# A pooling stage between two FFNs: boundary chain first on every engine, gate rows and weight low parts in its gaps, bias by float32r matmuls of two parts

## The chip, the cores and the metric

The kernel runs on one core of a Trainium2 chip. The metric is device time in microseconds of one execution; a kernel's time is the median of its runs. A profile is one further execution with the hardware profiler on.

## What is computed

A two-layer encoder trunk over 256 tokens of 1024 channels, all in float32. Each layer is FFN, token mixer, FFN. The mixer of layer 0 pools, that of layer 1 is latent attention. Every sub-layer has a norm before and after and is shifted, scaled and gated by rows computed from a vector `c`.

```python
def pool_mixer(h, w, b, scale):            # group g: window 2, 4, 8, 16; 256 channels each
    ...
    y = jnp.einsum('bsgc,gcd->bsgd', pooled - hg, w) + b
    return y.reshape(B, S, D_MODEL) * scale

def modulated_sublayer(x, mod, g_pre, g_post, fn, weight):
    shift, scale, gate = mod[:, 0], mod[:, 1], mod[:, 2]
    h = rmsnorm(x, g_pre) * (1.0 + scale) + shift
    y = rmsnorm(fn(h), g_post)
    return x + weight * (1.0 + gate) * y
...
    mod = (sc @ ada_w[i] + ada_b[i]).reshape(B, N_MOD, D_MODEL)[:, :, None, :]
```

## The kernel before

Tokens are two tiles of 128 (t = 0, 1), with x resident in SBUF. A product in float32 accuracy is made of three float32r matmuls: each operand is split into a high part (a cast on ScalarE, ACT) and a low part (operand minus high part, on VectorE, DVE), and TensorE (PE) adds high x high, high x low and low x high (`mm3`, lines L98 to L100). Weights arrive as 1 MB pieces: `wi` of the FFN's input (chunk c, half q of the inner dimension: wi00, wi01, wi10, ...), `wo` of its output, `ada` for the modulation rows. Each piece is a task of the class `Bulk`: load (a DMA on SP's queue into one of `N_RAW` = 4 raw buffers), high part, low part. When a piece's last work on DVE is written down, `advance()` writes the next load into SP's queue; that load then waits on the chip until DVE has read the buffer that it overwrites. The split parts lie in a ring of 12 buffers (`hl_tile`).

The modulation rows are made on DVE: `ada_step` (L352) adds one row of `ada_w` times a value of `c`. The tasks ("ada", 0, 7, 2) and ("ada", 0, 7, 3), ada2 and ada3 for short, are the last two pieces of the scale row of the next FFN.

The code order is the order on each engine; nothing is rescheduled, and each engine runs its instructions strictly in that order. SP's queue too is in code order.

A boundary between two sub-layers is a chain for each tile: sums of squares of the sub-layer's output on ACT (`post_sq`, L508), the norm's factor (`rstd`: DVE L501, then GpSimd L503), x updated on DVE (L535 to L538), squares of x on ACT (L508), factor again, x scaled into `xr` (one half on ACT L554, the other on DVE L555), transposed on PE (`turn_half`, L562, into `ps_h`), modulated into `hs` (one half on ACT L576, the other on DVE L582), split into `hTH` (L588, L590) and `hTL` (L593). The next matmuls need hTH and hTL.

The stage of the change lies between the first FFN `f0` and the second, `f2`. `FFN.tail` of f0 ends with tile 0's chain, during which tile 1's last matmuls run; its arguments `next_weights`, `between` and `between2` put extra work into it. Then the pooling: `pool_map` multiplies hT by the group weights `pw` into `z` (PE, L98 to L100), ACT copies z to SBUF (L1466, L1481, L1482), `pool_bias` puts the bias row into the accumulators `accp` by a plain float32 matmul with one row of ones (L954), `pool_mix` adds the pooling as a plain float32 matmul with the matrix `mix` (L965), `pool_scale_rows` multiplies by `pool_scale` into `pooly` (DVE, L979). `rows_of_gate` makes the gate row G (PE L448, DVE L456, L457), `reduce_held` sums rows over partitions by one-column matmuls (`ps_mod`, L361), and `warm` issues matmuls into a scratch bank that nobody reads (L108). Then follow tile 0's chain and `FFN.head` of f2, which starts with `in00` (chunk 0, tile 0) on PE while tile 1's chain runs. Constants of the stage, `mix`, `pool_b` and `pool_scale`, are loaded by `pool_consts` (L926, L928, L929); `pool_b` and `pool_scale` share the buffer `poolbs`.

Of the kernel before, what the change touches and what calls it, by code (L numbers as in the profile page):

```python
# [39 lines left out]
def kernel(  # L40
# [387 lines left out]
    def gate(layer, sub, hold=None, in_parts=True):  # L428
# [15 lines left out]
        def half(acc, dst, hf, ps, halves=None, staged=None):  # L444
# [10 lines left out]
            def after():  # L455
                nc.vector.tensor_add(dst[:, sl], ps if staged is None else dst[:, sl], rows[2 * hf])  # L456
                nc.vector.scalar_tensor_tensor(  # L457
                    dst[:, sl], dst[:, sl], 1.0, rows[2 * hf + 1], op0=ALU.add, op1=ALU.mult
                )
# [1220 lines left out]
```

## Time and profile before

| | |
|---|---|
| median of 3 runs | 925.95 us (924.56 to 929.2) |
| the profiled execution | 930.35 us, of which the span from its first to its last instruction is 928.6 us |
| mean granted TensorE clock | 0.990 |
| busy: PE, DVE, ACT, GpSimd | 97%, 76%, 47%, 5% of the span |
| DMA | 235.28 MB, mean 253 GB/s |

Rows of the timeline read: start, duration, engine, line, operation, tile written and tiles read, shape, count. A row x4 merges four records; a plain float32 matmul leaves two records. A bracket at a row's end is idle time of its engine in front of it, and what ended it. Adjacent records of one engine overlap a little, since one is issued before the other has drained.

### The profile page before, as it was taken

What the parts mean: (1) busy time and instruction counts of PE and PEld (TensorE: products, weight loads), DVE (VectorE), ACT (ScalarE), POOL (GpSimd) and SP (SyncE); (2) the same over time, 40 slices, a digit from 0 to 9 for tenths busy, and PEclk for the clock granted to TensorE, in tenths of its full rate; (3) what the DMA queues carried; (4) which work ended last, traced back from release to release, by engine and by line L of the source; (5) the groups of instructions that cost most, each with busy time, mean ns of one, the idle gap of its engine ahead of it and who ended that gap; (6) DMA issues with size and microseconds to landing.
All of it is one profiled execution on the core that took longest, in us unless ns stands there. A gap on an engine that the chain in (4) does not pass through costs nothing.

```text
span 928.6 us, 11171 instructions
## 1 busy us (share of the span) xinstructions
PE 898.9 (97%) x4251; PEld 733.0 (79%) x4251; DVE 703.9 (76%) x848; ACT 437.3 (47%) x653; POOL 41.8 (5%) x56
## 2 busy tenths in 40 slices
PE   3999999999999999999999999999999999999997
PEld 3568887887888888888888888888776888888885
DVE  5798888887877898797867987766798765656553
ACT  2255443345645434334742534337698654343421
POOL 0000000000000000000000000001163000000000
PEclk9899999999999999999999999998999999999999
DMA  9989998996357999898469999961143458857601
GB/s 325 368 299 343 360 373 313 351 359 242 137 180 264 378 339 326 297 387 275 137 183 360 324 351 327 344 229 59 46 137 113 160 153 280 293 193 259 227 1 45
DMA packets 135973, 235.28 MB, mean 253 GB/s; under 512 B 5628, under 2 KB 98415, under 8 KB 135664
## 3 DMA queue, kind: packets, MB, share of 16 engines
q1 hardware_dynamic: 135920, 234.58, 72.8%
q8 instruction: 33, 0.54, 0.2%
q14 instruction: 20, 0.16, 0.1%
HBM read 233.51 MB, written 1.05 MB: 253 GB/s over the span
## 4 chain that ended last, share of the span: by engine, by line
PE 88%; DVE 7%; issue 2%; DMA 1%; ACT 1%; POOL 0%; SPq 0%; DVEq 0%; POOLq 0%; ACTq 0%
PE acc L747 25%; PE in L100 16%; PE in L98 16%; PE in L99 16%; PE accm L1319 2%; PE ps_g L724 2%; DVE aacc L352 1%; PE ps_h L562 1%; PE ps_mod L361 1%; PE in L794 1%; DVE nm L1220 1%; DVE ql L1203 1%; DMA wo<-in_ffn_w_out_dram 1%; PE accp L965 1%; DMA adah<-in_ada_w_dram 1%
## 5 line engine op out<-in xcount | busy, mean ns | idle before, releaser
L352 DVE SCALAR_TENSOR_TENSOR aacc<-ada,sc,aacc 128x1024 f32<-128x1024 f32 (+1 forms) x113 | 143.8, 1272 | 9.9 <-DMA ada<-in_ada_w_dram 7.6
L708 ACT ACTIVATE sil<-in 128x256 f32<-128x256 f32 x84 | 32.2, 383 | 247.0 <-PE in L100 242.1
L710 DVE TENSOR_TENSOR g<-in,sil 128x256 f32<-128x256 f32 x84 | 35.2, 419 | 52.0 <-ACT sil L708 51.9
L95 DVE TENSOR_TENSOR gL<-ps_g,gH 128x256 fp32r<-128x256 f32 x88 | 36.6, 416 | 23.6 <-ACT gH L94 23.5
L94 ACT CAST gH<-ps_g 128x256 fp32r<-128x256 f32 x88 | 32.4, 368 | 44.5 <-PE ps_g L724 44.4
L503 POOL TENSOR_TENSOR r<-ms,mhalf 128x1 f32<-128x1 f32 x24 | 13.6, 565 | 840.5 <-DVE ms L501 840.5
L724 PEld LDWEIGHTS ps_g<-ident,g 128*128 128x128 f32 x176 | 24.7, 140 | 11.5
L724 PE MATMUL ps_g<-ident,g 128*128 128x128 f32 x176 | 33.6, 272 | 0.0
L508 ACT ACTIVATE junk<-x 128x512 bf16<-128x512 f32 x24 | 15.1, 631 | 21.1 <-DVE x L535 11.3
L361 PE MATMUL ps_mod<-ones,aacc 128*128 128x1 f32 x96 | 12.9, 262 | 10.9 <-DVE cols L150 9.7
L361 PEld LDWEIGHTS ps_mod<-ones,aacc 128*128 128x128 f32 x96 | 13.2, 213 | 11.9 <-DVE cols L150 10.0
L576 ACT ACTIVATE hs<-ps_h,mod,mod 128x128 f32<-128x128 f32 x48 | 18.0, 456 | 8.6 <-DVE mod L377 5.5
L352 DVE SCALAR_TENSOR_TENSOR aacc<-adah,sc,aacc 128x512 f32<-128x512 f32 x28 | 21.0, 751 | 0.9
L582 DVE TENSOR_SCALAR hs<-ps_h,mod,mod 128x128 f32<-128x128 f32 x48 | 16.4, 403 | 4.9 <-PE ps_h L562 4.6
L535 DVE SCALAR_TENSOR_TENSOR x<-tmp,r,x 128x512 f32<-128x512 f32 x23 | 16.3, 748 | 2.2 <-POOL r L503 1.2
L1238 POOL TENSOR_SCALAR p<-p,rs 128x256 f32<-128x256 f32 x16 | 16.1, 1008 | 26.8 <-ACT p L1228 16.4
L1228 ACT ACTIVATE p<-s,nm 128x256 f32<-128x256 f32 x32 | 15.0, 478 | 4.0 <-DVE nm L1220 2.6
L554 ACT ACTIVATE xr<-x,r 128x512 f32<-128x512 f32 x12 | 8.7, 722 | 17.4 <-POOL r L503 17.4
L593 DVE TENSOR_TENSOR hTL<-hs,hTH 128x512 fp32r<-128x512 f32 x24 | 15.6, 689 | 0.4
L271 DVE TENSOR_TENSOR wo10L<-wo,wo10H 128x2048 fp32r<-128x2048 f32 x4 | 9.2, 2292 | 8.1 <-ACT wo10H L263 8.1
L397 DVE TENSOR_REDUCE mod<-ps_turn 128x4 f32<-128x512 f32 x12 | 8.2, 687 | 8.1 <-PE ps_turn L391 8.1
L562 PE MATMUL ps_h<-ident,xr 128*128 128x128 f32 x96 | 13.7, 283 | 0.5 <-ACT xr L554 0.3
(498 smaller groups left out, 2880.3 us busy)
## 6 DMA issues: line engine op xcount, KB each, us to landing
wi<-in_ffn_w_in_dram SPq DMA_DIRECT2D x176, 512.0 KB, 5.8
ada<-in_ada_w_dram SPq DMA_DIRECT2D x64, 1024.0 KB, 7.1
wo<-in_ffn_w_out_dram SPq DMA_DIRECT2D x44, 1024.0 KB, 6.4
adah<-in_ada_w_dram SPq DMA_DIRECT2D x6, 1024.0 KB, 10.3
mwo<-in_mla_w_o_dram SPq DMA_DIRECT2D x4, 1024.0 KB, 6.1
bc<-in_ada_b_dram SPq DMA_DIRECT2D x12, 256.0 KB, 6.8
bc<-in_norm_g_dram SPq DMA_DIRECT2D x12, 256.0 KB, 7.4
adah<-in_ada_w_dram SPq DMA_DIRECT2D x4, 512.0 KB, 11.7
```

The costliest lines, as they stand in the source:

```text
L94: nc.scalar.copy(h, src)
L95: nc.vector.tensor_sub(lo, src, h.bitcast(F32))
L98: nc.tensor.matmul(ps, lhsT=lh, rhs=rh, start=first, stop=False)
L99: nc.tensor.matmul(ps, lhsT=lh, rhs=rl, start=False, stop=False)
L100: nc.tensor.matmul(ps, lhsT=ll, rhs=rh, start=False, stop=last)
L352: nc.vector.scalar_tensor_tensor(acc, w, sc[:, k : k + 1], acc, op0=ALU.mult, op1=ALU.add)
L361: nc.tensor.matmul(ps[:, j : j + 1], lhsT=acc[:, (j - j0) * P : (j - j0 + 1) * P], rhs=ones[:, 0:1], start=True, stop=True,)
L562: nc.tensor.transpose(ps[:, j * P : (j + 1) * P], xr[:, kk * P : (kk + 1) * P], ident)
L708: nc.scalar.activation(sil, ps[:, 0:CW], AF.Silu)
L710: nc.vector.tensor_mul(g, ps[:, CW : 2 * CW], sil)
L724: nc.tensor.transpose(ps[:, a * P : (a + 1) * P], g[:, a * P : (a + 1) * P], ident)
L747: nc.tensor.matmul(acc[hf], lhsT=lhs[:, a, :], rhs=rhs[:, a, hf * 512 : (hf + 1) * 512], start=f, stop=l)
```

## The change

It reorders the stage and changes a few forms. In f0's tail, the second ada2 piece is done earlier, `pool_consts` and the first quarter of ada3 come after it, and the new `pool_bias_split` splits the bias row into two float32r parts, which `pool_bias` then adds by two float32r matmuls for each half. Tile 1's chain goes ahead of the mixing on PE; high and low parts of wi00 and wi01, the gate rows and quarters of ada3 move into places between the chain's steps. `pre_scale` can give ACT the second half of `xr` (`act_half`), `mod_half` can let each engine cast its own half (`own`), and the first matmuls of every `FFN.head` take all high parts of hT first and the low part last (`low_last`). Most `warm` matmuls go.

```diff
@@ pre_scale, mod_half
-    def pre_scale(t, r):
+    def pre_scale(t, r, act_half=0):
         xr = rowp.tile([P, D], F32, tag="xr", name=f"xr{t}")
-        nc.scalar.activation(xr[:, 0:512], xt[t][:, 0:512], AF.Copy, scale=r)
-        nc.vector.tensor_scalar(xr[:, 512:1024], xt[t][:, 512:1024], r, None, op0=ALU.mult)
+        a, v = (slice(hf * 512, (hf + 1) * 512) for hf in (act_half, 1 - act_half))
+        nc.scalar.activation(xr[:, a], xt[t][:, a], AF.Copy, scale=r)
+        nc.vector.tensor_scalar(xr[:, v], xt[t][:, v], r, None, op0=ALU.mult)
...
-            if on_act:
+            if on_act != own:
                 nc.vector.tensor_copy(hh[:, bsl, :], hv)
@@ FFN.mm_in
+            if low_last:
+                todo = [(hh, i, k) for k in ks for i in range(2)] + [(hl, 0, k) for k in ks]
+                for n, (lhs, i, k) in enumerate(todo):
+                    rhs = self.wi[c, k // 4][i][:, k % 4, :]
+                    nc.tensor.matmul(ps, lhsT=lhs[:, k, :], rhs=rhs, start=n == 0 and k == 0, stop=False)
+                return
...
-            ps = self.inn(0, 0, hT0)
+            ps = self.inn(0, 0, hT0, low_last=True)
@@ pool_bias
-    def pool_bias(t):
-        acc = acc_tile(t, f"accp{t}")
-        for hf in range(2):
-            nc.tensor.matmul(
-                acc[hf],
-                lhsT=ones[0:1, :],
-                rhs=pool_st["bs"][0:1, hf * 512 : (hf + 1) * 512],
...
+    def pool_bias(t, acc, hf):
+        for i, part in enumerate(pool_st["b"]):
+            nc.tensor.matmul(
+                acc[hf], lhsT=ones_r[0:1, :], rhs=part[0:1, hf * 512 : (hf + 1) * 512], start=i == 0, stop=False
+            )
+
+    def pool_bias_split():
+        b = pool_st["bs"][0:1, 0:D]
+        hl = hl_tile("poolb")
+        bh, bl = hl[:, 0:D], hl[:, D : 2 * D]
+        nc.scalar.copy(bh[0:1, :], b)
+        nc.vector.tensor_sub(bl[0:1, :], b, bh[0:1, :].bitcast(F32))
+        pool_st["b"] = (bh, bl)
@@ the stage
-    def last_ada2():
+    def to_pool_map():
+        to_pool()
+        bulk.low_part(ada2, 0, 1, False)
+
+    def ahead():
         pool_consts()
-        bulk.low_part(ada2, 1, 2, True, 512, D)
+        bulk.low_part(ada3, 0, 1, False, 0, 512)
 
     hT0 = ffn_tail(
-        f0, hT, 0, 0, 0, 1, to_pool,
-        between=lambda: bulk.low_part(ada2, 0, 1, False),
-        between2=(lambda: bulk.low_part(ada2, 1, 2, False, 0, 512), last_ada2),
+        f0, hT, 0, 0, 0, 1, to_pool_map,
+        between=lambda: bulk.low_part(ada2, 1, 2, True),
+        between2=(ahead, pool_bias_split),
     )
...
-    rows_of_gate = held["pool"]([psum.tile([P, 512], F32, tag="in", name=f"ps_row{hf}") for hf in range(2)])
-    rows_of_gate([0])
-    accp0 = pool_bias(0)
+    nc.scalar.copy(*z0[1])
+    bulk.low_part(ada3, 0, 1, False, 512, D)
+    rows_of_gate = held["pool"](acc_tile(1, "ps_row"))
+    r = rstd(s2, 1.0)
+    rows_of_gate([0], (0,))
+    xr = pre_scale(1, r, 1)
+    bulk.low_part(ada3, 1, 2, False, 0, 512)
+    accp0 = acc_tile(0, "accp0")
+    for hf in range(2):
+        pool_bias(0, accp0, hf)
+    hT1 = new_hT(1)
+    h0, l0, _ = mod_half(1, 0, turn_half(1, 0, xr), hT1, 0, 1, False, True)
+    h1, l1, _ = mod_half(1, 1, turn_half(1, 1, xr), hT1, 0, 1, True, True)
     pool_mix(accp0, 0, 0)
...
+    bulk.low_part(wi(0, 0), 0, 2048, True)
     pool_mix(accp0, 0, 1)
-    pool_mix(accp1, 1, 0, (2, 3))
+    after = [reduce_held(0, 6, psum.tile([P, 512], F32, tag="in", name="ps_mod06"))]
+    accp1 = acc_tile(1, "accp1")
+    pool_bias(1, accp1, 0)
+    pool_bias(1, accp1, 1)
+    after += [reduce_held(0, 7, psum.tile([P, 512], F32, tag="in", name="ps_mod07"))]
+    pool_mix(accp1, 1, 0)
     pool_mix(accp1, 1, 1)
-    more = warm(0, "in", 2)
-    after = [reduce_held(0, 6)]
-    more(2)
-    after += [reduce_held(0, 7)]
-    more(6)
     y0 = pool_scale_rows(0, accp0)
...
+    bulk.low_part(wi(0, 1), 0, 1024, False)
+    r = rstd(s2, 1.0)
     y1 = pool_scale_rows(1, accp1, (0,))
-    xr = pre_xr(0, s2)
+    xr = pre_scale(0, r, 1)
...
+    warm(2, "in", 2)
+    h0()
+    h1()
+    l0()
+    l1()
+    ss = post_sq(y1, 1.0)
+    bulk.low_part(wi(0, 1), 1024, 2048, True)
+    f2.high_in(1, 0)
```

On SP's queue, in f0's tail, the loads stood so before (wi_1575 is wi00, wi_1617 is wi01, wi_1704 is wi10; ada_1517 is ada2 and ada_1569 is ada3):

```order
L291 DMA ada_1517<-in_ada_w_dram 128x2x1024
L291 DMA ada_1569<-in_ada_w_dram 128x2x1024
L626 DMA wi_1575<-in_ffn_w_in_dram 128x4x256 x2
L626 DMA wi_1617<-in_ffn_w_in_dram 128x4x256 x2
L926 DMA mix<-in_mix_dram 128x2x1024
L928 DMA poolbs<-in_pool_b_dram 1x1024
L929 DMA poolbs<-in_pool_scale_dram 128x1024
L626 DMA wi_1704<-in_ffn_w_in_dram 128x4x256 x2
```

And now, with wi_1673 as wi10:

```order
L629 DMA wi_1575<-in_ffn_w_in_dram 128x4x256 x2
L629 DMA wi_1617<-in_ffn_w_in_dram 128x4x256 x2
L629 DMA wi_1673<-in_ffn_w_in_dram 128x4x256 x2
L935 DMA mix<-in_mix_dram 128x2x1024
L937 DMA poolbs<-in_pool_b_dram 1x1024
L938 DMA poolbs<-in_pool_scale_dram 128x1024
```

The load of wi10 moved from behind the three constants to in front of them; the buffer that it waits for is ada2's.

On ACT, at the end of f0's tail, the cast of tile 0's `hs` and its modulation stood right behind the last gH before:

```order
L94 CAST gH_1693<-ps_g_1690 128x256
L576 ACTIVATE hs_1720<-ps_h_1715,mod_674,mod_952 128x128 x4
L590 CAST hTH_1713<-hs_1730 128x512
L508 ACTIVATE junk,ss<-acc_0_566 128x512
L508 ACTIVATE junk,ss<-acc_1_567 128x512
```

Now:

```order
L94 CAST gH_1703<-ps_g_1700 128x256
L966 CAST poolb<-poolbs 1x1024
L579 ACTIVATE hs_1723<-ps_h_1718,mod_674,mod_952 128x128 x4
L593 CAST hTH_1716<-hs_1733 128x512
L510 ACTIVATE junk,ss<-acc_0_566 128x512
```

The cast of the bias row stands between gH and `hs`; on DVE the subtraction L967 stands likewise between gL and `hs`.

On DVE, behind tile 0's modulation for f2, there stood before:

```order
L582 TENSOR_SCALAR hs_1996<-ps_h_1991,mod_1933,mod_1921 128x128 x4
L588 CAST hTH_1979<-hs_1986 128x512
L593 TENSOR_TENSOR hTL_1980<-hs_1986,hTH_1979 128x512
L593 TENSOR_TENSOR hTL_1980<-hs_1996,hTH_1979 128x512
L271 TENSOR_TENSOR wi10L<-wi_1704,wi10H 128x2048
L523 TENSOR_TENSOR tmp_2041<-pooly,G_1800 128x512
```

Now:

```order
L585 TENSOR_SCALAR hs_1977<-ps_h_1972,mod_1925,mod_1909 128x128 x4
L591 CAST hTH_1970<-hs_1977 128x512
L596 TENSOR_TENSOR hTL_1971<-hs_1977,hTH_1970 128x512
L596 TENSOR_TENSOR hTL_1971<-hs_1987,hTH_1970 128x512
L271 TENSOR_TENSOR wi01L<-wi_1617,wi01H 128x1024
L271 TENSOR_TENSOR wi10L<-wi_1673,wi10H 128x2048
```

Half of wi01's low part moved in between. The high part of wi10, which ACT cast ahead of the boundary chain before, now stands on ACT behind that chain and the two squares of `pooly`.

## Rows read from the trace of the kernel before

**Rows 1.** The page: busy time by engine; chain that ended last, by engine.

```profile
PE 898.9 (97%) x4251; PEld 733.0 (79%) x4251; DVE 703.9 (76%) x848; ACT 437.3 (47%) x653; POOL 41.8 (5%) x56
...
PE 88%; DVE 7%; issue 2%; DMA 1%; ACT 1%; POOL 0%; SPq 0%; DVEq 0%; POOLq 0%; ACTq 0%
```

**Rows 2.** Windows: us, busy by engine (instructions), granted clock, DMA share, GB/s.

```profile
234.00:240.00 6.00, 5.82 (x28) 4.20 (x27) 5.52 (x9) 4.53 (x7) 0.00 (x0) 0.84 0.04 6
240.00:246.00 6.00, 6.00 (x29) 5.37 (x28) 5.22 (x6) 3.83 (x6) 0.18 (x1) 0.88 1.04 345
```

**Rows 3.** Timeline of PE in the stage.

```profile
224.87 0.28 PE L98 MATMUL z<-pwH,hTH 128*128 128x256 f32 x1
...
229.63 1.98 PE L954 MATMUL accp<-poolbs,ones 1*128 1x512 f32 x4
...
254.55 0.50 PE L98 MATMUL in<-wi00H,hTH 128*128 128x512 f32 x1 [0.45 <-DVE hTH L588]
...
266.40 1.10 PE L562 MATMUL ps_h<-ident,xr 128*128 128x128 f32 x8
```

**Rows 4.** Timeline of DVE, from f0's tail to f2's head.

```profile
216.86 1.28 DVE L352 SCALAR_TENSOR_TENSOR aacc<-ada,sc,aacc 128x1024 f32<-128x1024 f32 x1
...
221.43 0.74 DVE L352 SCALAR_TENSOR_TENSOR aacc<-ada,sc,aacc 128x512 f32<-128x512 f32 x1
222.32 1.37 DVE L582 TENSOR_SCALAR hs<-ps_h,mod,mod 128x128 f32<-128x128 f32 x4
223.60 0.42 DVE L588 CAST hTH<-hs 128x512 fp32r<-128x512 f32 x1
...
230.95 0.49 DVE L555 TENSOR_SCALAR xr<-x,r 128x512 f32<-128x512 f32 x1 [0.67 <-POOL r L503]
...
243.11 0.69 DVE L979 TENSOR_TENSOR pooly<-accp,poolbs 128x512 f32<-128x512 f32 x1
...
250.22 0.48 DVE L555 TENSOR_SCALAR xr<-x,r 128x512 f32<-128x512 f32 x1 [0.66 <-POOL r L503]
...
255.74 2.28 DVE L271 TENSOR_TENSOR wi10L<-wi,wi10H 128x2048 fp32r<-128x2048 f32 x1
...
261.07 2.29 DVE L271 TENSOR_TENSOR wi11L<-wi,wi11H 128x2048 fp32r<-128x2048 f32 x1
...
263.61 1.22 DVE L271 TENSOR_TENSOR wo0L<-wo,wo0H 128x1024 fp32r<-128x1024 f32 x1
```

**Rows 5.** Timeline of ACT, from f0's tail into the stage.

```profile
207.86 1.91 ACT L263 CAST pwH<-pw 128x2048 fp32r<-128x2048 f32 x1
...
220.66 0.35 ACT L94 CAST gH<-ps_g 128x256 fp32r<-128x256 f32 x1
221.88 1.50 ACT L576 ACTIVATE hs<-ps_h,mod,mod 128x128 f32<-128x128 f32 x4 [0.87 <-PE ps_h L562]
...
227.94 0.58 ACT L1466 COPY poolz<-z 128x512 f32<-128x512 f32 x1 [0.85 <-PE z L100]
228.42 0.63 ACT L508 ACTIVATE junk<-x 128x512 bf16<-128x512 f32 x1
```

**Rows 6.** Timeline of SP's DMA queue; the duration is that of the issue.

```profile
213.90 0.50 SPq L926 DMA_DIRECT2D mix<-in_mix_dram  x1
214.44 0.32 SPq L928 DMA_DIRECT2D poolbs<-in_pool_b_dram  x1
...
222.20 0.92 SPq L626 DMA_DIRECT2D wi<-in_ffn_w_in_dram  x2
```

**Rows 7.** A half-microsecond window; DMA issues (KB each, us to landing).

```profile
226.50:227.00 0.50, 0.50 (x6) 0.50 (x5) 0.44 (x2) 0.50 (x1) 0.14 (x1) 1.00 0.45 156
...
wo<-in_ffn_w_out_dram SPq DMA_DIRECT2D x1, 1024.0 KB, 5.8
bc<-in_ada_b_dram SPq DMA_DIRECT2D x2, 256.0 KB, 6.3
...
c_col<-in_c_dram SPq DMA_DIRECT2D x1, 4.0 KB, 1.8
```

More of the change, by code (lines that the diff above doesn't have):

```diff
@@ L453, in half, with after @@
                 staged.append(lambda: nc.scalar.copy(dst[:, sl], ps))
[L455 to L459, printed above, removed]
+            def after(steps=(0, 1)):
+                if 0 in steps:
+                    nc.vector.tensor_add(dst[:, sl], ps if staged is None else dst[:, sl], rows[2 * hf])
+                if 1 in steps:
+                    nc.vector.scalar_tensor_tensor(
+                        dst[:, sl], dst[:, sl], 1.0, rows[2 * hf + 1], op0=ALU.add, op1=ALU.mult
+                    )
             return after
@@ L471, in finish, with after @@
             afters = [half(acc, dst, hf, banks[hf], staged=staged) for hf in range(2)]
-            def after(halves):
+            def after(halves, steps=(0, 1)):
                 for hf in halves:
-                    afters[hf]()
+                    afters[hf](steps)
             return after
@@ L563, in turn_half, with mod_half @@
         return ps
-    def mod_half(t, hf, ps, hT, layer, sub, on_act):
+    def mod_half(t, hf, ps, hT, layer, sub, on_act, own=False):
         A, B = mods[layer, 3 * sub + 1], mods[layer, 3 * sub]
@@ L1459 @@
     )
     acc1 = f0.acc[1]
-    z0 = pool_map(0, hT0)
+    wi = lambda c, q: ("wi", 0, 1, c, q)
+    z0 = [pool_map(0, hT0, hf) for hf in range(2)]
     r = post_norm(1, acc1, 0.5, mods[0, 2])
-    for dst, src in z0:
-        nc.scalar.copy(dst, src)
+    nc.scalar.copy(*z0[0])
     s2 = post_add(1, acc1, r, mods[0, 2])
-    rows_of_gate = held["pool"]([psum.tile([P, 512], F32, tag="in", name=f"ps_row{hf}") for hf in range(2)])
-    rows_of_gate([0])
-    accp0 = pool_bias(0)
-    pool_mix(accp0, 0, 0)
@@ new lines @@
+    accp0 = acc_tile(0, "accp0")
[4 more added lines that the diff above has]
+    h1, l1, _ = mod_half(1, 1, turn_half(1, 1, xr), hT1, 0, 1, True, True)
+    pool_mix(accp0, 0, 0)
+    h0()
+    h1()
+    l0()
+    rows_of_gate([1], (0,))
+    l1()
+    z1 = [pool_map(1, hT1, hf) for hf in range(2)]
+    f2.high_in(0, 0)
+    nc.scalar.copy(*z1[0])
+    nc.scalar.copy(*z1[1])
+    bulk.high_part(wi(0, 1), 0, 1024)
@@ new lines @@
+    bulk.high_part(wi(0, 1), 1024, 2048)
+    bulk.low_part(ada3, 1, 2, True, 512, D)
+    for hf in range(2):
+        rows_of_gate([hf], (1,))
+    bulk.low_part(wi(0, 0), 0, 2048, True)
+    pool_mix(accp0, 0, 1)
+    after = [reduce_held(0, 6, psum.tile([P, 512], F32, tag="in", name="ps_mod06"))]
[4 more added lines that the diff above has]
+    pool_mix(accp1, 1, 0)
@@ L1497 @@
+    pool_mix(accp1, 1, 1)
+    y0 = pool_scale_rows(0, accp0)
+    G = mods[0, 5]
+    r = post_norm(0, y0, 1.0, G, (0,))
+    s2 = post_add(0, y0, r, G)
+    bulk.low_part(wi(0, 1), 0, 1024, False)
+    r = rstd(s2, 1.0)
     y1 = pool_scale_rows(1, accp1, (0,))
-    xr = pre_xr(0, s2)
-    pool_scale_rows(1, accp1, (1,))
-    ss = post_sq(y1, 1.0)
+    xr = pre_scale(0, r, 1)
     for f in after:
         f()
-    hT0 = pre(0, xr, 0, 2)
-    more(6)
+    pool_scale_rows(1, accp1, (1,))
+    hT0 = new_hT(0)
```

55 lines of the change are left out of this document (19 added, 36 removed).

## The prediction

> **What bounds the kernel now.** I read the page first: TensorE (PE) is busy for 97% of the span and makes 88% of the chain that ended last, VectorE (DVE) 7% [rows 1]. So time is lost where PE stands still, or does work that another order would hide. Next I read the stretches around the pooling stage. It lies between the first `z` matmul at 224.87 us and the first `in` matmul of the next FFN at 254.55 us [rows 3]. The granted clock averages 0.84 and 0.88 in 234 to 246 us: of its two levels, 2.4 and 1.2 GHz, the lower one ran for (0.16 x 6 + 0.12 x 6) / 0.5 = 3.4 us of those [rows 2]. Then I read the timelines of PE, DVE, ScalarE (ACT) and the DMA queue on SP, because the change reorders all four [rows 3 to 6], and how long loads take to land [rows 7]. PE hardly waits in this stage. It fills it with work that multiplies no weights: plain float32 bias rows, `ps_mod` sums, `warm`. The path that sets the end is x, norm, transposes, hT, and on it DVE and ACT run strictly in their written order.
>
> **Part 1, the late constant.** This term decides. The split of `pool_b` puts a cast on ACT ahead of `hs` of token tile 0, and a subtraction on DVE ahead of the other half of `hs`. Both need the landing of the `pool_b` DMA. Before, `mix` was issued at 213.90 and `pool_b` at 214.44 us, with only wi01 ahead [rows 6], and nobody needed it before the bias matmul at 229.63 [rows 3]. Now ada2 ends earlier in the code, so the load of wi10 stands on SP ahead of `mix` and `pool_b`. That load waits until DVE has read the raw buffer of ada2. The last read is now an L352 of the same width at the place of the one at 216.86 us, which ends at 218.14 [rows 4]. Before, the same release took 0.03 us: the L352 ended at 222.17, wi10 was issued at 222.20 [rows 4, 6]. So wi10 goes out near 218.17, takes the queue 0.92 us, `mix` takes 0.50 [rows 6], and `pool_b` is issued near 219.7: 5.3 us later than before.
>
> When does it land? The 1 MB of wi10 issued at 222.20 kept the DMA engines moving into the stretch up to 227.0, about 4.7 us with its start-up [rows 6, 7]. `mix` is another 1 MB; at 345 GB/s, the rate of a stretch in which the engines are always busy [rows 2], that is 3.0 us. 218.17 + 4.7 + 3.0 = 225.9, if the 4 KB wait their turn. Do they? A `bc` load of 256 KB, issued next behind a 1 MB `wo`, landed 6.3 us after issue where the `wo` took 5.8, so it came behind it and not past it. Against that, a 4 KB load on an idle queue took 1.8 us [rows 7]. Bounds: 221.5 and 227. I take 225.9, since two big transfers stand ahead as in the `bc` row. The Trainium skill says the same of the order, in DMA: Bandwidth & Descriptors, section "Queues, rings and completion order": on each DMA engine descriptors are consumed in ring order. The same page, section "Anatomy of one DMA", gives a transfer about 2.0 us fixed plus its bytes; by that alone the landing would be 221.7 and the result that of the first rival below.
>
> ACT reaches the cast when gH ends, at 221.0, and then stands until 225.9 [rows 5]. No row here has such a cast 1024 wide; half of the 1.91 us of a 2048-wide one is about 1.0 [rows 5] (bounds 0.6, a 512-wide copy, and 1.9; one partition instead of 128 is taken as no gain). The subtraction is taken as the 1.22 us of a 128x1024 one, up to 0 if one partition were free [rows 4]. So DVE's `hs`, which began at 222.32, begins at 225.9 + 1.05 + 1.2 = 228.2. Its 1.37 us and 0.34 of the cast to hTH follow [rows 4], and `z` can start at 230.0 instead of 224.87. **PE stands still for 5.1 us.**
>
> **Part 2, what the new order gives back inside the stage.** I followed the printed order engine by engine with the durations of the same rows.
> - Tile 1's `xr` was at 230.95 [rows 4]. DVE is 5.9 us late there, and ACT saves 1.0, since the squares no longer wait for the second `z` copy at 227.94 [rows 5]: 236.0, +5.0.
> - Its transposes no longer stand behind a plain float32 bias (1.98 us for two matmuls [rows 3]) and `mix`. For the two-part float32r bias no row has one partition; it lies between half of 1.98 and 1.98, and I take half. PE has slack there either way. That brings `z` of tile 1 to an end near 242.
> - `pooly` on DVE was at 243.11 [rows 4]. Now gate rows, an ada piece and the low part of wi00 stand in front: 245.0, +1.9.
> - From `pooly` to tile 0's `xr` it is 7.1 us (243.11 to 250.22) as before: 252.2. The transposes then start at once, without `ps_mod` and `warm` in front, and in00 starts at 255.6 instead of 254.55: +1.05. So 4.05 of the 5.1 us are back.
>
> **Part 3, what is lost again behind it.** Before, DVE went from hTL straight to wi10L at 255.74 [rows 4]. Now the second half of wi01L (1.22 us [rows 4]) stands there, and wi10L needs wi10H, which ACT casts only after hTH and two squares of some 0.7 us: 257.6 + 1.9 = 259.5 [rows 5]. So wi10L is 3.8 us late. wi11L, which went straight into PE's use before, comes near 264.4 instead of 261.07 [rows 4]. PE waits for it, tile 1's `xr` is late by as much, and the transposes that were at 266.40 [rows 3] come near 269.7: **+3.3 us** in place of +1.05. What follows, the loads of weights included, hangs on these and shifts along; a PE that is 97% busy has no idle to absorb it. That the low parts of hT come last in in00 saves at most the 0.45 us in front of it [rows 3], which is in this sum.
>
> **Part 4, the clock.** Before, it fell once, inside 234 to 246 us [rows 2], after float32 and one-row matmuls with short waits. 3.4 us at the lower level are 1.7 us of PE work. Now there is a standstill of 5.1 us, and later two `ps_mod` groups with only bias rows between them and no `warm`. Bounds: 0, if PE's slack hides all, and about 5.5 for long stretches at both places. I take 1.7: one such stretch more than now that shows.
>
> **Sum.** 5.1 - 4.05 + 2.25 + 1.7 = +5.0 us. The profiled execution took 930.35 us, its span of 928.6 and 1.75 around it; it lies 4.4 above the median of the runs, 925.95. The sum is a difference between spans and is added to the median: 931.0 us.
>
> **The rivals.**
> - *`pool_b` passes what is queued ahead* (not slower). It lands 1.8 us after issue, at 221.5; cast and subtraction end near 223.8 and `z` starts at 225.5: 0.6 - 4.05 + 2.25 and 0.5 for the clock is -0.7: 925.2 us. It decides from a landing before about 222.5. The 1.8 us row speaks for it, the `bc` row against it. Chance 0.12.
> - *DVE is not the bound behind the stage*: the stall stands, part 3 costs nothing: +1.05, 927.0 us. For it: wi10 lands long before, so ACT's cast could fit a gap. Against: wi11L had nothing to spare before. Chance 0.12.
> - *The clock stays low at both places*: 3.3 + 5.5, 934.8 us. The fall of the clock before needed less than a standstill; for the length only one stretch of 3.4 us speaks [rows 2]. Chance 0.12. The Trainium skill has a rule for it, TensorE: Matmul & The Clock Gate, section "HAM oscillation — how this bites in real kernels": waits between bursts of matmuls send the clock back to the lower level, and each burst starts slow. By that rule the time is this rival's; the fall before came with hardly any wait, so the trace can't tell [rows 2].
> - *No stall and no DVE bound*: in00 starts 3.4 us early and keeps it: 922.5 us. Chance 0.04.
>
> **How the numbers follow.** The forecast has 0.60, and a range of its own of 928.5 to 933.5. For 8 in 10 I go down to 925.4, just over the first rival, and up to 935.0. Within 0.5% (4.6 us, about what a measurement of this kernel tells from no change) reaches to 930.6. Of the forecast's 0.60, 0.35 lie above that; with the clock's rival slower has 0.47. Faster by over 0.5% needs less than 921.3: a tail of the last rival and what I have not seen, 0.05. The rest, 0.48, is no change.
>
> **What would show it.** Part 1: an ACT row of the cast with some 5 us idle before it, released by the DMA of `poolbs`, and PE idle before `z`. Part 2: in00 near 255 to 257. Part 3: DVE waiting for ACT before wi10L, PE waiting for wi11L. Part 4: granted clock below 1 after 228 and again between 244 and 256. The forecast is wrong if the cast starts before 222.5, or if tile 1's transposes, 266.40 before, are not later.

## The result, and the profile after

The changed kernel took 938.67 us (median of 4 runs, 938.28 to 939.65) where the kernel before took 925.25 (4 runs, 924.26 to 929.2): ratio 1.0114, 95% interval 1.0086 to 1.0143, about 10.5 us slower (8 to 13 by the interval; the two medians themselves lie 13.4 apart). The forecast was 931.0, 5 us slower, with a range up to 935.0; the sign was right and the size was half of what the ratio says. The profiled execution took 939.65 us, its span 937.9.

The page of the changed kernel, as in [rows 1]: PE is as long busy as before in a longer span, and its share of the chain fell from 88 to 85%.

```profile
PE 898.9 (96%) x4227; PEld 733.9 (78%) x4227; DVE 705.3 (75%) x851; ACT 438.4 (47%) x655; POOL 41.7 (4%) x56
...
PE 85%; DVE 8%; DMA 2%; issue 2%; ACT 2%; POOL 1%; SPq 0%; DVEq 0%; POOLq 0%; ACTq 0%
```

SP's queue and ACT of the changed kernel, to set against [rows 5, 6]. `pool_b` goes out at 219.07 instead of 214.44, behind wi10 and `mix`, and the cast waits 6.00 us for it:

```profile
217.51 0.92 SPq L629 DMA_DIRECT2D wi<-in_ffn_w_in_dram  x2
218.48 0.50 SPq L935 DMA_DIRECT2D mix<-in_mix_dram  x1
219.07 0.27 SPq L937 DMA_DIRECT2D poolbs<-in_pool_b_dram  x1
```

```profile
226.35 1.04 ACT L966 CAST poolb<-poolbs 1x1024 fp32r<-1x1024 f32 x1 [6.00 <-DMA poolbs<-in_pool_b_dram]
...
262.98 1.89 ACT L263 CAST wi10H<-wi 128x2048 fp32r<-128x2048 f32 x1
```

PE's timeline, against [rows 3]:

```profile
230.30 0.58 PE L950 MATMUL z<-pwH,hTH 128*128 128x256 f32 x1 [5.97 <-DVE hTH L591]
...
246.35 1.84 PE L361 MATMUL ps_mod<-ones,aacc 128*128 128x1 f32 x16
248.12 1.20 PE L958 MATMUL accp<-poolb,ones 1*128 1x512 f32 x4
249.25 2.95 PE L361 MATMUL ps_mod<-ones,aacc 128*128 128x1 f32 x16
252.06 6.04 PE L972 MATMUL accp<-poolz,mix 128*128 128x256 f32 x16
258.41 1.09 PE L565 MATMUL ps_h<-ident,xr 128*128 128x128 f32 x8 [0.32 <-DVE xr L558]
...
261.19 0.47 PE L709 MATMUL in<-wi00H,hTH 128*128 128x512 f32 x1 [1.24 <-DVE hTH L591]
...
272.59 0.50 PE L99 MATMUL in<-wi11L,hTH 128*128 128x512 f32 x1 [2.32 <-DVE wi11L L271]
...
276.81 1.27 PE L565 MATMUL ps_h<-ident,xr 128*128 128x128 f32 x8
```

DVE's, against [rows 4]:

```profile
228.56 1.35 DVE L585 TENSOR_SCALAR hs<-ps_h,mod,mod 128x128 f32<-128x128 f32 x4
...
237.62 0.48 DVE L558 TENSOR_SCALAR xr<-x,r 128x512 f32<-128x512 f32 x1
...
247.33 1.28 DVE L986 TENSOR_TENSOR pooly<-accp,poolbs 128x512 f32<-128x512 f32 x2
...
257.27 0.69 DVE L986 TENSOR_TENSOR pooly<-accp,poolbs 128x512 f32<-128x512 f32 x1 [3.30 <-PE accp L972]
257.88 0.48 DVE L558 TENSOR_SCALAR xr<-x,r 128x512 f32<-128x512 f32 x1
...
262.34 1.22 DVE L271 TENSOR_TENSOR wi01L<-wi,wi01H 128x1024 fp32r<-128x1024 f32 x1
264.91 2.29 DVE L271 TENSOR_TENSOR wi10L<-wi,wi10H 128x2048 fp32r<-128x2048 f32 x1 [1.35 <-ACT wi10H L263]
...
270.25 2.29 DVE L271 TENSOR_TENSOR wi11L<-wi,wi11H 128x2048 fp32r<-128x2048 f32 x1
```

And the windows, with the granted clock in the third column from the right, against [rows 2]:

```profile
228.00:234.00 6.00, 3.70 (x17) 3.70 (x18) 5.90 (x13) 3.40 (x10) 0.55 (x1) 0.62 0.00 0
234.00:240.00 6.00, 6.00 (x26) 4.08 (x25) 3.30 (x8) 2.40 (x6) 0.55 (x1) 0.81 0.00 0
240.00:246.00 6.00, 6.00 (x39) 5.37 (x39) 5.93 (x11) 5.72 (x9) 0.00 (x0) 1.00 0.13 29
246.00:252.00 6.00, 6.00 (x39) 5.47 (x38) 4.74 (x7) 3.15 (x7) 0.55 (x1) 0.83 0.93 323
252.00:258.00 6.00, 6.00 (x17) 4.67 (x17) 2.67 (x6) 1.64 (x5) 0.55 (x1) 0.60 0.00 1
...
270.00:276.00 6.00, 3.68 (x13) 2.71 (x12) 5.27 (x7) 2.20 (x6) 0.55 (x1) 0.82 0.65 213
276.00:282.00 6.00, 6.00 (x30) 5.09 (x29) 4.17 (x10) 4.35 (x8) 0.00 (x0) 0.89 0.76 250
```

Read them in the order of time, changed kernel less kernel before. `z` is 5.43 us late (5.1 forecast). Tile 1's `xr` is 6.67 late, tile 0's 7.66, in00 6.64 (1.05 forecast), tile 1's transposes 10.41 (3.3 forecast). Those of tile 0 came 0.7 us sooner than before (220.57 and 221.24 in the two timelines), so the stage as a whole lost 11.1. By the prediction's own formula, (1 - clock) x 6 / 0.5 summed over the windows, the lower level ran here for 4.6 + 2.3 + 2.0 + 4.8 + 2.2 + 1.3 = 17.2 us, against 3.4. I call such a time at the lower level a low stretch; the clock in it is half, so it costs at most half its length. The two spans differ by 9.3 and not by 11.1, since outside the stage each execution has low stretches of its own: 14.7 us before and 8.5 in the changed kernel. Behind the transposes of tile 1 the two take 662.2 and 661.1 us (7.8 and 5.3 of them at the lower level), so that `low_last`, which also changed the heads of the later FFNs, shows no loss there.

The table, from each kernel's timeline of PE, sets the executions side by side: starts in us behind the transposes of tile 0, the time at the lower level from 222 to 282 us, by the same formula from windows of 6 us, and the ratio to the kernel before, timed beside it.

| kernel | z | in00 | transposes, tile 1 | low clock | ratio (95%) |
|---|---|---|---|---|---|
| before | 3.6 | 33.3 | 45.2 | 3.4 | |
| before_again | 3.6 | 34.9 | 46.7 | 6.7 | |
| after | 9.7 | 40.6 | 56.2 | 17.2 | 1.0114 (1.0086, 1.0143) |
| change_again | 9.1 | 39.2 | 55.0 | 16.9 | 1.0091 (1.0055, 1.0127) |
| consts_first | 3.6 | 30.6 | 46.4 | 6.8 | 1.0021 (1.0009, 1.0034) |
| plain_bias | 3.6 | 33.3 | 49.1 | 10.2 | 1.0032 (1.0012, 1.0053) |
| b_before_mix | 6.1 | 37.0 | 51.4 | 13.6 | 1.0052 (1.0021, 1.0083) |
| fill_stall | 8.5 | 35.3 | 51.1 | 6.7 | 1.0078 (1.0056, 1.0100) |
| old_tail | 8.3 | 36.4 | 51.0 | 6.8 | 1.0072 (1.0051, 1.0093) |
| fill_both | 8.5 | 37.8 | 52.2 | 6.8 | 1.0068 (1.0044, 1.0092) |
| heads_late_const | 8.6 | 39.7 | 51.6 | 13.6 | 1.0057 (1.0038, 1.0076) |
| wi10_sooner | 3.6 | 33.6 | 46.6 | 10.2 | 1.0003 (0.9986, 1.0020) |
| heads_early | 4.6 | 33.3 | 45.1 | 6.8 | 0.9980 (0.9966, 0.9995) |
| best3 | 3.6 | 31.6 | 43.7 | 3.5 | 0.9988 (0.9975, 1.0001) |
| best1 | 3.6 | 30.3 | 42.7 | 3.4 | 0.9969 (0.9955, 0.9983) |
| no_sums | 4.3 | 30.9 | 43.3 | 3.4 | 0.9954 (0.9939, 0.9969) |
| no_sums_best | 3.7 | 30.3 | 42.7 | 6.7 | 0.9961 (0.9945, 0.9978) |

### The profile page after: what moved, and what is told of

Same layout as the page of the kernel before. It is cut to its first block, busy times and chain, and to the rows that moved or that the text cites. A ratio compares the mean times of both kernels' runs of the same rounds, so it can differ in the third digit from the quotient of the medians.

```text
span 937.9 us, 11135 instructions
## 1 busy us (share of the span) xinstructions
PE 898.9 (96%) x4227; PEld 733.9 (78%) x4227; DVE 705.3 (75%) x851; ACT 438.4 (47%) x655; POOL 41.7 (4%) x56
## 3 DMA queue, kind: packets, MB, share of 16 engines
HBM read 233.51 MB, written 1.05 MB: 250 GB/s over the span
## 4 chain that ended last, share of the span: by engine, by line
PE 85%; DVE 8%; DMA 2%; issue 2%; ACT 2%; POOL 1%; SPq 0%; DVEq 0%; POOLq 0%; ACTq 0%
PE acc L756 25%; PE in L100 15%; PE in L99 15%; PE in L98 15%; PE accm L1326 2%; PE ps_g L733 2%; DVE aacc L352 1%; PE ps_mod L361 1%; PE ps_h L565 1%; PE in L803 1%; PE accp L972 1%; PE z L950 1%; DVE nm L1227 1%; DVE ql L1210 1%; DMA poolbs<-in_pool_b_dram 1%
## 5 line engine op out<-in xcount | busy, mean ns | idle before, releaser
L352 DVE SCALAR_TENSOR_TENSOR aacc<-ada,sc,aacc 128x1024 f32<-128x1024 f32 (+1 forms) x114 | 144.1, 1264 | 11.8 <-DMA ada<-in_ada_w_dram 9.6
L719 DVE TENSOR_TENSOR g<-in,sil 128x256 f32<-128x256 f32 x84 | 35.3, 421 | 52.1 <-ACT sil L717 52.0
L579 ACT ACTIVATE hs<-ps_h,mod,mod 128x128 f32<-128x128 f32 x48 | 18.0, 454 | 14.6 <-PE ps_h L565 8.7
L361 PE MATMUL ps_mod<-ones,aacc 128*128 128x1 f32 x96 | 13.3, 266 | 11.2 <-DVE cols L150 10.5
L565 PE MATMUL ps_h<-ident,xr 128*128 128x128 f32 x96 | 14.4, 292 | 0.8 <-DVE xr L558 0.3
## 6 DMA issues: line engine op xcount, KB each, us to landing
adah<-in_ada_w_dram SPq DMA_DIRECT2D x6, 1024.0 KB, 11.1
```

The source lines that it names most:

```text
L352: nc.vector.scalar_tensor_tensor(acc, w, sc[:, k : k + 1], acc, op0=ALU.mult, op1=ALU.add)
L361: nc.tensor.matmul(ps[:, j : j + 1], lhsT=acc[:, (j - j0) * P : (j - j0 + 1) * P], rhs=ones[:, 0:1], start=True, stop=True,)
L565: nc.tensor.transpose(ps[:, j * P : (j + 1) * P], xr[:, kk * P : (kk + 1) * P], ident)
L719: nc.vector.tensor_mul(g, ps[:, CW : 2 * CW], sil)
```

## The experiments

**consts_first.** The loads of the constants ahead of the step that releases wi10:

```diff
-        between=lambda: bulk.low_part(ada2, 1, 2, True),
+        between=lambda: (pool_consts(), bulk.low_part(ada2, 1, 2, True)),
...
     def ahead():
-        pool_consts()
```

> The changed kernel with one move: the loads of mix, pool_b and pool_scale stand on SP ahead of the VectorE step that releases the load of wi10, so that pool_b is issued near 213 instead of 219.1 us and has landed before ScalarE reaches its cast at 220.4. Theory 1, the late constant is the root, and the low clock of 229 to 236 and of 250 to 257 us comes from the standstill: ScalarE waits less than 0.5 us for the cast, z starts at 225 to 226 instead of 230.3, the two stretches at the lower clock go or shrink to one of 3.4 us, and the time falls by 8 to 14 us to 924 to 930. Theory 2, the low clock comes from what PE does in this stage (float32 sums, one-row bias, no warm matmuls) and not from the standstill: the 5.4 us at z come back, the stretches stay, 932 to 935. Theory 3, pool_b lands late for another reason: no difference, 938 to 939.

ACT's cast, the mix of tile 1 and the wait behind in00:

```profile
218.34 1.04 ACT L966 CAST poolb<-poolbs 1x1024 fp32r<-1x1024 f32 x1
```

```profile
240.88 5.27 PE L972 MATMUL accp<-poolz,mix 128*128 128x256 f32 x16
...
260.64 0.50 PE L99 MATMUL in<-wi11L,hTH 128*128 128x512 f32 x1 [2.32 <-DVE wi11L L271]
```

The cast waits for nothing, and `z` stands where it stood before. The ratio falls to 1.0021, clear of both measurements of the change: most of the loss hangs on the late load. In us the fall is 0.0070 to 0.0093 of 928, 6.5 to 8.6, by which of the two it is taken from; theory 1 wanted 8 to 14. What stays is a low stretch of 3.4 us in the mix, so that theory 2 holds for that one, and the 2.32 us for wi11L with another of 3.5 behind it.

**plain_bias.** The cast and the subtraction gone, the bias as before the change:

```diff
-        between2=(ahead, pool_bias_split),
+        between2=(ahead, nop),
...
-        for i, part in enumerate(pool_st["b"]):
-            nc.tensor.matmul(
-                acc[hf], lhsT=ones_r[0:1, :], rhs=part[0:1, hf * 512 : (hf + 1) * 512], start=i == 0, stop=False
-            )
+        nc.tensor.matmul(
+            acc[hf], lhsT=ones[0:1, :], rhs=pool_st["bs"][0:1, hf * 512 : (hf + 1) * 512], start=True, stop=False
+        )
```

> The changed kernel without the split of pool_b: the bias is again one plain float32 matmul per half, the cast on ScalarE and the subtraction on VectorE are gone, and the loads stay as late as they are. Nothing ahead of z needs pool_b; the first to need it is the bias near 229.5 us, after its landing at 226.3. Theory 1 (late constant is the root): z at 224.9, time within 2 us of the kernel that loads the constants first, so 924 to 930; the dearer bias, about 1 us more per token tile than the split one, shows in PE's slack. Theory 2 (clock by the mix of work): the bias in float32 makes it no better, 932 to 936.

1.0032, `z` 3.6 us behind the transposes although the loads are as late as in the changed kernel. So it is the wait of work that stands ahead of `hs`, not the late load in itself, that costs. The interval overlaps that of consts_first, and the median, 931.25 us, lies between the ranges of the two theories (924 to 930 and 932 to 936), 1.4 us behind consts_first. Theory 1 fits the place of `z` and the distance to consts_first.

**b_before_mix.** In pool_consts the load of `pool_b` stands ahead of that of `mix`:

```diff
-        nc.sync.dma_start(mx.rearrange("p (a n) -> p a n", a=NT), mix.rearrange("(a p) n -> p a n", p=P))
         bs = hl_tile("poolbs", F32)
         nc.sync.dma_start(bs[0:1, 0:D], pool_b[0:1].rearrange("l g n -> l (g n)"))
+        nc.sync.dma_start(mx.rearrange("p (a n) -> p a n", a=NT), mix.rearrange("(a p) n -> p a n", p=P))
```

> The changed kernel with the 4 KB load of pool_b ahead of the 1 MB of mix on SP, both still behind the load of wi10. Theory 1 (a small load lands in the order of the queue, behind the megabytes ahead of it): pool_b lands with wi10 near 223, the cast waits 2.5 to 3.5 us instead of 6.0, z starts at 226.5 to 227.5, and the time falls by 3 us for the wait and 0 to 3 for the clock: ratio to before 1.004 to 1.009. Theory 2 (it passes what is queued, and 226 came from a slow path of its own): it lands about as long after its issue as before, 7 us, cast at 225 to 225.7, ratio 1.010 to 1.012.

```profile
221.86 1.05 ACT L966 CAST poolb<-poolbs 1x1024 fp32r<-1x1024 f32 x1 [2.31 <-DMA poolbs<-in_pool_b_dram]
```

Issued at 217.69, it is there 4.2 us later instead of 7.3: one megabyte ahead of it instead of two. That is theory 1, a little sooner than it said. The cast does not wait for `pool_scale`, the other load into `poolbs`: that stands behind `mix`, which landed only near 225.3 in this run. By the ratio about half of the excess over 1 is left, but the five times spread from 928.5 to 935.3 us and the interval overlaps that of change_again.

**fill_stall.** PE's standstill filled:

```diff
+    warm(22, "in", 2)
     z0 = [pool_map(0, hT0, hf) for hf in range(2)]
```

> The changed kernel with 22 warm matmuls (5.5 us of PE at 0.25 us each) put where PE stands still between the last out matmul and z. The standstill of the path stays: z still at 230 to 230.5. Theory 1 (the low clock after 229 us follows from PE's idling): granted clock 1.00 in 228 to 240, xr of tile 1 near 236 instead of 237.6, in00 near 255.6 to 258 instead of 261.2, time down by 3 to 6 us to 933 to 936. Theory 2 (the mix of work): clock low again in 229 to 240, time 938 to 939.5.

```profile
228.00:234.00 6.00, 5.77 (x34) 4.01 (x32) 5.60 (x12) 4.27 (x11) 1.09 (x2) 1.00 0.01 3
234.00:240.00 6.00, 6.00 (x42) 5.54 (x43) 5.84 (x12) 4.78 (x9) 0.00 (x0) 1.00 0.00 0
...
246.00:252.00 6.00, 5.68 (x21) 4.42 (x21) 4.28 (x10) 2.17 (x5) 0.55 (x1) 0.72 0.13 54
```

`z` is still 4.8 us late, but the clock is full at 228 to 240, and in00 stands at 35.3 instead of 40.6: the first low stretch follows from PE's standing still, as theory 1 has it. One of 3.4 us stays in the mix. In time it is 1.0078, 1.2 to 3.3 us better than the two measurements of the change, where theory 1 said 3 to 6; the intervals overlap, so the gain in time is not shown.

**old_tail.** PE's tail as before the change:

```diff
-    after = [reduce_held(0, 6, psum.tile([P, 512], F32, tag="in", name="ps_mod06"))]
...
-    after += [reduce_held(0, 7, psum.tile([P, 512], F32, tag="in", name="ps_mod07"))]
     pool_mix(accp1, 1, 0)
     pool_mix(accp1, 1, 1)
+    more = warm(0, "in", 2)
+    after = [reduce_held(0, 6)]
+    more(2)
+    after += [reduce_held(0, 7)]
+    more(6)
...
-    warm(2, "in", 2)
+    more(6)
```

> The changed kernel with PE's tail as it was before the change: both ps_mod sums behind the last mix matmul of tile 1, with 2 and 6 warm matmuls between and behind them and 6 behind the transposes. The late constant stays. Theory 1 (the second stretch at the lower clock, 250 to 257 us, comes from the sums with only one-row work between them): the mix of tile 1 runs at the full clock, VectorE's wait of 3.3 us for it goes, in00 at 258 to 259.5, time down 2 to 3 us to 935.5 to 937. Theory 2 (the second stretch follows from the first, whatever order stands there): the sums themselves then fall into it, in00 at 261 to 262, time 938 to 940.

```profile
244.00 3.72 PE L972 MATMUL accp<-poolz,mix 128*128 128x256 f32 x16
```

```profile
246.00:252.00 6.00, 6.00 (x48) 5.79 (x48) 4.92 (x12) 2.31 (x7) 1.10 (x2) 1.00 0.36 147
```

The mix of tile 1 takes 3.72 us instead of 6.04, DVE does not wait for it, and no second low stretch comes: theory 1. The ratio, 1.0072, is 1.8 to 3.9 us below the change, with overlapping intervals.

**heads_early.** consts_first, and behind in00 two moves:

```diff
     r = rstd(s2, 1.0)
+    bulk.low_part(wi(0, 1), 1024, 2048, True)
     y1 = pool_scale_rows(1, accp1, (0,))
     xr = pre_scale(0, r, 1)
+    f2.high_in(1, 0)
...
     ss = post_sq(y1, 1.0)
-    bulk.low_part(wi(0, 1), 1024, 2048, True)
-    f2.high_in(1, 0)
```

> The kernel that loads the constants first, with two more moves: the second half of the low part of wi01 stands on VectorE ahead of pooly of tile 1 (a gap of 1.6 us in that kernel) instead of behind hTL, and the cast of wi10 stands on ScalarE in its gap ahead of hs (2.5 us) instead of behind hTH and four squares. Theory 1 (what is left of the loss is VectorE's and ScalarE's work behind in00): wi10L starts right behind hTL, PE's wait of 2.32 us for wi11L shrinks below 0.5 us, the low stretch at 261 to 264.5 us goes, the transposes of tile 1 come 2 to 4 us sooner, ratio to before 0.996 to 0.999 in place of 1.002. Theory 2 (the loss is in the order of the low parts in in00, or in the clock alone): the wait stays or moves to another weight, ratio 1.001 to 1.003.

```profile
262.03 0.50 PE L99 MATMUL in<-wi11L,hTH 128*128 128x512 f32 x1 [0.21 <-DVE wi11L L271]
```

The wait is all but gone, tile 1's transposes come 11.8 us behind in00 as before (15.8 in consts_first), and the ratio is 0.998, clear of the 1.0021 of consts_first: theory 1. Part 3's cause is shown. In this execution in00 itself stands 2.7 us later than in consts_first: the cast waited 0.90 us for `pool_b`, and the low stretch at the mix was 6.8 us long instead of 3.4.

**wi10_sooner.** consts_first, with ACT's cast alone moved:

```diff
-    ss = post_sq(y1, 1.0)
     bulk.low_part(wi(0, 1), 1024, 2048, True)
     f2.high_in(1, 0)
+    ss = post_sq(y1, 1.0)
```

> The kernel that loads the constants first, with ScalarE's cast of wi10 ahead of the four squares of pooly of tile 1, and nothing else. Theory 1 (VectorE's wait of 1.35 us for that cast is what makes wi11L late, and the extra 1.22 us of wi01 that stand ahead are hidden): wi10L 1.3 us sooner, PE's wait for wi11L about 1.0 instead of 2.32 us, ratio 0.9985 to 1.001 in place of 1.002. Theory 2 (the squares are late instead, and chain 1 with wi11L waits for them): no gain, 1.001 to 1.003.

PE's wait for wi11L is 1.35 instead of 2.32 us, in00 to the transposes 13.0. So about 1 us of that wait is ACT's cast behind the two squares of `pooly` (four rows on ACT, since each square is followed by the read of its sum), the rest the half of wi01 on DVE. The ratio, 1.0003 (0.9986, 1.0020), fits theory 1 but cannot be told from 1.0021.

**heads_late_const.** The changed kernel with the two moves of heads_early and the constants left late.

> The changed kernel with the late constant left as it is, and only the two moves behind in00 (second half of the low part of wi01 ahead of pooly of tile 1, cast of wi10 ahead of hs). Theory 1 (the loss behind in00 is additive, 3 to 4 us as in the kernels with the constants first): PE's wait of 2.32 us for wi11L goes below 0.5, ratio 0.003 to 0.005 below that of the changed kernel in this call. Theory 2 (behind a late head the work has slack): within 0.001 of it.

1.0057 where the changed kernel timed beside it had 1.0091: 3.2 us less, and 11.8 us from in00 to the transposes, with a wait of 0.20 us. The two intervals overlap; the times are 931.4 to 936.1 against 935.6 to 938.7. The loss behind in00 adds to that in front of it: theory 1.

**best1** is heads_early with both sums behind the mix of tile 1, as in old_tail but without its warm matmuls; **best3** is best1 with them, and with both halves of tile 1's `pooly` behind `xr`.

> The kernel with constants first and both moves behind in00, and besides both ps_mod sums behind the mix of tile 1 on PE, with no warm matmuls added. Theory 1 (the clock falls where sums and one-row work stand ahead of the mix): the mix of tile 1 runs at the full clock and ends 2.5 us sooner, pooly of tile 1 waits for nothing; what the sums cost is hidden while PE waits for xr; ratio to before 0.994 to 0.998. Theory 2 (the sums behind the mix bring the low clock there, and the transposes and in00 run in it): 1 to 2 us worse than with the sums ahead, 0.998 to 1.001.

> As the kernel before it in this call, but with the warm matmuls of the kernel before the change between and behind the sums and behind the transposes, and both halves of pooly of tile 1 behind xr of tile 0. Theory 1 (warm matmuls keep the clock): granted clock 1.00 from 220 to 280 us, in00 at the same place as without them or up to 0.5 us later, ratio to before 0.993 to 0.997. Theory 2 (they change nothing, and cost PE time): 0.5 to 1 us slower than without them.

best1 has the lowest ratio of those that compute everything, 0.9969 (0.9955 to 0.9983), 2.9 us faster than the kernel before; the interval overlaps that of heads_early. Its mix takes 3.72 us, yet a low stretch of 3.4 us comes behind the sums, in 246 to 252 us, so both theories have a part. best3 has one of 3.5 there as well (0.95 and 0.76 from 240 to 252 us): the warm matmuls did not keep the clock, which is theory 2. Its ratio is no better, but it moved `pooly` too, so the time does not price the warm matmuls alone.

**change_again.** The changed kernel without an edit.

> The changed kernel itself, beside the kernel before on the chip of this call, so that the steps can be set against it. If the size of the loss is one of the change: ratio to before 1.010 to 1.013, as measured first. If part of it came from where it ran (the cast waited 6.0 us for pool_b there and 4.5 us in the two kernels that fill PE, which leave the loads alone): 1.007 to 1.010, with the cast at 223.3 to 224.5 us.

```profile
226.29 1.04 ACT L966 CAST poolb<-poolbs 1x1024 fp32r<-1x1024 f32 x1 [5.41 <-DMA poolbs<-in_pool_b_dram]
```

1.0091 lies in the range of the second theory, but the cast began at 226.29 and not at 223.3 to 224.5, so its mechanism did not show. The first ratio, 1.0114, lies inside this interval: a loss of 8 to 11 us is the change's own, and its size is known no better. The kernel before had medians of 928.0 to 928.9 us in the later runs (13 to 26 executions each), so the four that gave 925.25 stand low.

**fill_both.** fill_stall and old_tail together.

> The changed kernel with both covers for the clock: 22 warm matmuls in PE's standstill ahead of z, and PE's tail of the kernel before (sums behind the mix, with its warm matmuls). The late constant and the order on VectorE and ScalarE stay. Theory 1 (the loss is the sum of waits as forecast, +3.3, and the rest is the clock at two places): no low stretch from 222 to 260 us, ratio to before 1.002 to 1.005. Theory 2 (the covers mend the same loss once): as either of them alone, 1.007 to 1.008.

```profile
246.00:252.00 6.00, 6.00 (x44) 5.90 (x43) 4.97 (x11) 2.17 (x5) 0.89 (x2) 0.86 0.26 104
252.00:258.00 6.00, 6.00 (x33) 5.95 (x32) 2.91 (x7) 2.03 (x5) 0.00 (x0) 0.57 0.00 0
```

1.0068, no better than either alone: theory 2. The first low stretch is gone; the second came nevertheless, for 6.8 us, behind the mix (3.72 us), among the sums and in spite of the warm matmuls.

**no_sums** and **no_sums_best** are heads_early and best1 with this edit in the helper that sums a modulation. They leave out seven of the eight sums of each of two modulations, so they do not compute the network; they only price the sums:

```diff
-            for j in js:
+            for j in js if (layer, m) not in ((0, 6), (0, 7)) else ():
                 nc.tensor.matmul(
...
+            if (layer, m) in ((0, 6), (0, 7)):
+                nc.tensor.matmul(ps[:, j0 : j0 + n], lhsT=acc[:, 0:P], rhs=ones[:, 0:n], start=True, stop=True)
```

> The kernel with constants first and both moves behind in00, with the sums of the two modulations left out but for one matmul each (all eight columns get the sum of the first): 14 one-column float32 matmuls less ahead of the mix of tile 1, about 3.3 us of PE. Theory 1 (the one-column sums bring the second fall of the clock): no low stretch from 236 to 258 us, the mix of tile 1 ends 4 to 6 us sooner, ratio to before 0.993 to 0.996 in place of 0.998. Theory 2 (the fall has another cause: the one-row bias, or what PE did before): 3.4 us or more at the lower level remain there, ratio 0.996 to 0.998.

> The kernel that has the sums behind the mix besides, with the same sums left out but for one matmul each. PE then stands still some 4 to 5 us between the mix of tile 1 and the transposes of tile 0. Theory 1 (the sums bring the fall): none from 236 to 258 us, ratio 0.994 to 0.997. Theory 2 (PE's idling brings it as well): a low stretch of 3.4 to 7 us from about 246 us, in which in00 runs, ratio 0.997 to 0.999.

Windows and two rows of no_sums, then windows of no_sums_best:

```profile
234.00:240.00 6.00, 6.00 (x37) 5.18 (x37) 6.00 (x8) 4.89 (x6) 0.00 (x0) 1.00 0.55 162
240.00:246.00 6.00, 3.23 (x15) 2.50 (x14) 4.71 (x9) 2.54 (x8) 0.89 (x2) 1.00 0.54 191
246.00:252.00 6.00, 4.02 (x17) 3.56 (x18) 5.15 (x14) 4.71 (x8) 1.12 (x1) 0.72 0.51 175
```

```profile
239.53 3.70 PE L974 MATMUL accp<-poolz,mix 128*128 128x256 f32 x16
247.76 1.97 PE L567 MATMUL ps_h<-ident,xr 128*128 128x128 f32 x8 [4.53 <-DVE xr L560]
```

```profile
240.00:246.00 6.00, 1.48 (x10) 1.29 (x9) 5.68 (x12) 2.28 (x6) 1.67 (x2) 0.86 0.26 97
246.00:252.00 6.00, 5.79 (x21) 4.88 (x21) 5.19 (x10) 5.83 (x11) 0.00 (x0) 0.58 0.49 165
```

Without the sums the clock is full until the mix has ended (3.70 us); it is low once PE has stood still for 4.5 us waiting for `xr`, since the transposes behind that take 1.97 us instead of 1.09. The other runs agree on the mix: in all nine executions with both sums ahead of it it took 5.26 to 6.67 us, with the plain bias too, and in the six with the sums behind it or left out 3.70 to 3.72. So the sums bring the fall inside the mix, and standing still brings one too. no_sums has the ratio of theory 1, though not a clear 236 to 258 us; no_sums_best has the low stretch of theory 2 (6.7 us) and the ratio of theory 1.

**before_again.** The kernel before, profiled a second time.

> The kernel before the change, a second profile. Theory 1 (its one low stretch of 3.4 us at 238 us belongs to its order of work): again one stretch near 238, 3.4 us, give or take one more of that length. Theory 2 (the second fall comes and goes from execution to execution in any order): none, or one at 246 to 256 us.

```profile
234.00:240.00 6.00, 5.82 (x29) 5.10 (x28) 5.97 (x7) 3.44 (x4) 0.00 (x0) 0.72 0.31 92
240.00:246.00 6.00, 6.00 (x36) 5.44 (x34) 4.83 (x7) 3.97 (x8) 0.55 (x1) 1.00 1.04 374
246.00:252.00 6.00, 6.00 (x43) 6.00 (x43) 2.86 (x9) 3.21 (x10) 0.55 (x1) 0.76 0.16 63
252.00:258.00 6.00, 5.59 (x30) 4.46 (x29) 5.38 (x9) 5.25 (x7) 0.00 (x0) 0.96 0.02 4
```

There is one low stretch at the same place as in [rows 2] and another behind its sums that the first profile did not have: 6.7 us by windows. Both theories in part; the base of the forecast moves by some 1.6 us from execution to execution.

## Why the prediction was wrong

**Part 1** was right in its mechanism, and nearly in its size. The cast was forecast for 225.9 and began at 226.35, `hs` for 228.2 and 228.56, `z` for 230.0 and 230.30. Behind the transposes of tile 0, `z` came 6.1 us later than before in this execution and 4.6 to 5.5 later in the five others that leave both megabytes ahead; 5.1 were forecast. b_before_mix settles the rival in which the 4 KB pass the queue: they land behind what is issued ahead of them. The Trainium skill's rule, in DMA: Bandwidth & Descriptors, section "Queues, rings and completion order", that each DMA engine takes descriptors in ring order, agrees with these two landings. The other figure that the prediction took from that page of the Trainium skill, section "Anatomy of one DMA", is fitted there to loads issued by GpSimd; its 221.7 us did not come true for this load, which SP issued behind two others. From its issue to the cast it took 7.3 us here and 5.8 to 6.7 in the five others.

**Part 4** is the term that failed: "I take 1.7: one such stretch more than now that shows." The lower level ran for 17.2 - 3.4 = 13.8 us more, which is up to 6.9 us of PE work. By the sum below the lower level took 6.7 to 7.0 us of the path here; in the kernel before its one stretch hardly touched the path, where tile 0's `pooly` waited 0.17 us for PE. The upper bound, 5.5, was too low as well, since there were three places and I had seen two: behind the standstill (gone in fill_stall and consts_first), in the mix of tile 1 (gone in old_tail and in no_sums) and behind the wait for wi11L (gone with it in heads_early; with that wait it came in five of eight executions). The timed executions agree: the mean granted clock of change_again is 0.986, that of the kernel before beside it 0.993, and (1 - clock) times the span is 12.9 and 6.6 us, so that up to 6.3 us of its loss are the clock's. What I called the rival *The clock stays low at both places*, 934.8 us at a chance of 0.12, comes nearest to what happened, with the third place on top.

**Part 2** failed with it, at "From `pooly` to tile 0's `xr` it is 7.1 us (243.11 to 250.22) as before". It took 10.55 us (247.33 to 257.88). On DVE the first half of tile 1's `pooly` stands ahead of that `xr` in both kernels. But on PE the mix that this `pooly` needs now stands behind both sums, where before it stood ahead of them. In the kernel before that mix ended at 246.5, 1.9 us before `pooly` began, and `xr` waited for POOL alone [rows 4]:

```profile
240.92 5.61 PE L965 MATMUL accp<-poolz,mix 128*128 128x256 f32 x24
```

```profile
248.47 0.68 DVE L979 TENSOR_TENSOR pooly<-accp,poolbs 128x512 f32<-128x512 f32 x1
```

Now there is no such slack, and `pooly` waited 3.30 us for a mix at the lower level. That wait is the clock's: it is about half of the low stretch there, 3.30 of 6.8 us here, 1.64 and 1.65 of 3.4 in consts_first and fill_stall, and without it, in old_tail, the step takes 7.3 us. From `z` to in00 fill_stall takes 26.8 us, against 29.7 before and 25.6 forecast; less its wait of 1.65 that is 25.2, an estimate for the full clock. So what the order gives back was sized nearly right; the clock took it again.

**Part 3** named the right waits, and nearly their size: wi10L waited 1.35 us for ACT, PE 2.32 us for wi11L. From in00 to the transposes it took 15.6 instead of 11.85 us, 3.8 more where 2.25 were forecast. In b_before_mix, old_tail and fill_both, with the same wait and the full clock behind it, it took 14.4 to 14.6, so the waits cost 2.5 to 2.7. The rest, 1.0 to 1.3, is the third low stretch (0.82 and 0.89 at 270 to 282 us are 3.5 us of it, up to 1.7 us of work). heads_early and heads_late_const rule out the rival *DVE is not the bound*.

**The sum**, from the transposes of tile 0 on: 6.1 late at `z`; 4.5 given back (29.7 - 25.2); the clock's 2.4 ahead of tile 0's `pooly` (17.0 us behind `z` here, 14.6 in fill_stall) and 3.3 in the mix; 3.8 behind in00, of which 1.0 to 1.3 are the clock's: 6.1 - 4.5 + 2.4 + 3.3 + 3.8 = 11.1. Forecast: 5.1 - 4.05 + 1.7 + 2.25 = 5.0. In the forecast's terms the stall is 1.0 more, the waits behind in00 0.3 to 0.5 more, what came back 0.5 more, and the clock 6.7 to 7.0 where 1.7 were put. A rival on the other side, no stall and no DVE bound, was given 922.5 us, 3.45 below the median: heads_early takes both away and gains 1.9, best1, with the sums behind the mix besides, 2.9.
